# w_down by Strassen's seven products with weight sums made in DRAM, tanh gates, and differential heads in natural layout

## The chip, the cores and the metric

The kernel runs on one core of a Trainium2 chip. The metric is the device time of one execution in microseconds. Before the change it is 731.5 us, the median of 3 runs (731.49 to 732.18).

The engines are called by their short names in quoted rows: PE is TensorE (matmuls and transposes; PEld its weight loads, which overlap the matmuls), DVE is VectorE, ACT is ScalarE, POOL is GpSimd, SP only issues transfers. Every engine works through its instructions in order and waits at each for what that instruction needs.

## The reference

One decoder layer in float32 on x of shape (1, 512, 1024):

```
h = RMSNorm(x)
z = h @ w_in  ->  SWA q,k,v | differential q,k,v | gate logits gA, gB
yA = sliding-window attention (window 128, 8 heads, sinks)
ob[h] = (softmax(q1 k1) - lam * softmax(q2 k2)) @ v       4 heads of 128 columns, causal
yB = RMSNorm(ob) * subln * (1 - lam_init)                 per token and head
merged = sigmoid(gA) * (yA @ w_br_a) + sigmoid(gB) * (yB @ w_br_b)
x = x + merged @ w_o
u = causal depthwise conv3(RMSNorm(x) @ w_up) + b         2 x 2816 channels
x = x + (silu(ug) * uv) @ w_down                          2816 -> 1024
```

## The kernel before

Every operand of a large matmul is split in two parts, a high part rounded to the format that TensorE multiplies in one pass (fp32r) and the low rest. `mm3` (L143) issues three matmuls for a product of two blocks of 128: high x high, high x low, low x high. Weights are stored as units of 128 x 1024 in one DRAM tensor, in the order in which they are used (`worder`, L128). `wunit` (L135) keeps one unit ahead of the one in use: `split_unit` (L118) loads 512 KB through SP's queue into one of three buffers `raw`, ACT writes the high part `whi` and VectorE or POOL the low part `wlo`, both in three buffers. So a unit's split waits until TensorE has finished with the unit three before it, and its load waits until the split of the unit three before it is done.

TensorE's order is written out by hand (`manual_schedule`). In attention a stream of dense matmuls (gates, projections for the differential heads, branch A) is put between the steps of the attention units; the table `FILL` (L63) says how many steps of the stream follow each. The order of ACT, VectorE and POOL comes from the scheduler of the framework.

Four places matter here.

Gates. `gate(c)` (L465) evacuates a block of gate logits. `sigmoids` (L485) then applies the sigmoid to eight blocks at once; the first eight are held behind the last operations of sliding-window attention, the other eight behind the last exponentials of the differential heads. ACT keeps one set of function tables, and Sigmoid and Exp are in different ones: a load of tables stands before each change. `br_a` (L475) and `mix` (L848) multiply by the gates.

Differential heads. There are 16 units of a head and a block of 128 queries. `diff_score` makes the difference of the two softmaxes, `diff_trans` transposes it into one wide buffer for each head, and `diff_av` (L717) makes the product of a whole head, with the features on the partitions: twelve matmuls of 512 to 256 columns. The RMS norm over the features is then a sum over partitions: `token_sums` (L168) makes it with small matmuls against ones, and `along_free` (L183) spreads the factor over the partitions with eight diagonal matrices and two matmuls.

The up projection. 44 chunks of 128 channels, each from one weight unit of 24 matmuls; `conv` (L912) evacuates a chunk, applies the convolution, and after each pair of chunks the SiLU and the product, whose high part ACT writes and whose low part POOL.

The down projection (L965 to L974). Eight chunks of 128 output features; each takes three weight units and 22 products of `mm3` over 512 tokens, except that the last chunk is done in two halves of 256 tokens. VectorE adds x1, the residual, which lies with features on partitions, and ACT issues the store.

Of the kernel before, what the change touches and what calls it, by code (L numbers as in the profile page):

```python
# [11 lines left out]
F32 = mybir.dt.float32  # L12
# [46 lines left out]
U_N = U_DN + 8 * 3  # L59
# [3 lines left out]
FILL = dict(v=[9, 17, 25, 33], m=[0, 0, 0, 0], r=[4, 9, 13, 18], o=[7, 11, 15, 17], e=[1, 1, 0, 40], kv=4, up=3,  # L63
            warm=8, q=7, k=19, k2=4, s1=[0, 3, 2, 2, 2, 3, 3, 0, 0, 3], s2=[4, 3, 0, 3, 1, 7, 5, 2, 0, 1],
            s3=[3, 0, 1, 5, 6, 2, 2, 6, 0, 1], p0=4, p1=5, p2=8, ud=6, pd=[8, 9], f=[9, 0],
            a=[5, 1, 8, 7, 10, 2, 0, 3, 0, 1, 7, 4, 6, 0, 0, 5],
            b=[6, 2, 4, 4, 2, 7, 2, 1, 2, 0, 2, 0, 1, 1, 2, 2], c=[7, 0, 0, 1], d=[1, 0, 0, 5])
# [5 lines left out]
def tile_decoder_layer(ctx: ExitStack, tc: tile.TileContext, x4, wall, cst_d, relb_d, oneh_d, xn_d, out):  # L73
# [44 lines left out]
    def split_unit(i, width, eng):  # L118
        raw = wraw.tile([P, 1024], F32, tag="raw", name=nm("raw"))
        nc.sync.dma_start(raw[:, :width], wall[i][:, :width])  # L120
# [6 lines left out]

    worder = [u + i for u, n in ((U_QA, 4), (U_KV, 2), (U_GATE, 3), (U_DA, 4), (U_GATE + 3, 5), (U_VB, 4), (U_BRA, 4),  # L128
                                 (U_DB, 4), (U_GATE + 8, 8), (U_BRB, 4), (U_WO, 8), (U_UP, 2 * NF), (U_DN, 24))
              for i in range(n)]  # L130
    pooled = {u + i for u, n in ((U_DA, 4), (U_VB, 4), (U_DB, 4), (U_BRA, 4), (U_GATE, 16), (U_BRB + 3, 1)) for i in range(n)}
# [3 lines left out]
    def wunit(u):  # L135
        while wnext[0] < len(worder) and wnext[0] <= worder.index(u) + AHEAD:
            v = worder[wnext[0]]
            width = (DFF - 2 * 1024) if v >= U_DN and (v - U_DN) % 3 == 2 else 1024
# [4 lines left out]
    def mm3(ps, a, b, start, stop):  # L143

        nc.tensor.matmul(ps, a[0], b[0], start=start, stop=False)  # L145
        nc.tensor.matmul(ps, a[0], b[1], start=False, stop=False)  # L146
        nc.tensor.matmul(ps, a[1], b[0], start=False, stop=stop)  # L147
# [281 lines left out]
    def k_parts(ps, g):  # L429
# [5 lines left out]
        for k, (s, _) in zip(kh, halves):  # L435
            nc.scalar.activation(k[s, :], ps[s, :], AF.Copy, scale=g[s])
        for k, l, (s, o) in zip(kh, kl, halves):
            nc.vector.tensor_copy(k[o, :], k[s, :].bitcast(F32))
# [26 lines left out]
    def gate(c):  # L465
# [6 lines left out]
        nc.vector.tensor_tensor(t, ps, rbc, ALU.mult)  # L472
        G[c] = t

    def br_a(cp):  # L475
        w = wunit(U_BRA + cp)
        for j in range(2):
# [5 lines left out]
            nc.vector.tensor_tensor(G[c], ps, G[c], ALU.mult)  # L483

    def sigmoids(c0):  # L485
        return [nc.scalar.activation(G[c], G[c], AF.Sigmoid) for c in range(c0, c0 + 8)]
# [71 lines left out]
    swa_acts = []  # L558

    def swa_score(b, n):  # L560
# [22 lines left out]
        swa_acts.append(nc.scalar.activation(sk, sk, AF.Exp))  # L583
# [3 lines left out]
        for j in range(4):  # L587
            nc.vector.tensor_scalar(s[:, j, :W], s[:, j, :W], rc[:, j:j + 1], None, ALU.mult)
# [17 lines left out]
    def swa_av(b, n):  # L606
# [13 lines left out]
        if n == 1:  # L620
            qsl = slice(b * P, (b + 1) * P)
            uv = u.rearrange("p (j q) -> p j q", j=4)
            swa_acts.append(nc.scalar.activation(yah[:, :, qsl], uv, AF.Copy))
# [35 lines left out]
    exps = []  # L659

    def diff_score(h, b):
# [20 lines left out]
        for c in range(2):  # L682
            exps.append(nc.scalar.activation(p[:, c, :N], p[:, c, :N], AF.Exp, bias=nmx[:, c:c + 1],
                                             accum_out=sm[:, c:c + 1]))
# [3 lines left out]
        nc.vector.tensor_scalar(p[:, 1, :N], p[:, 1, :N], rc[:, 1:2], None, ALU.mult)  # L688
# [3 lines left out]
    def diff_trans(h, b):  # L692
        p = dp.pop((h, b))
        if b == 0:


            ath = at3.tile([P, 1664], F32R, tag="ath", name=nm("ath"), bufs=1)
            atl = at3.tile([P, 1664], F32R, tag="atl", name=nm("atl"), bufs=1)
            nc.gpsimd.memset(ath[:, 1408:1536].bitcast(F32), 0.0)
# [360 lines left out]
```

## Time and profile before

| what | us |
|---|---|
| median of 3 runs | 731.5 |
| the profiled execution | 730.34 |
| its span, first to last instruction | 728.6 |
| TensorE busy | 705.9 (97%) |
| VectorE busy | 450.0 (62%) |
| ACT busy | 316.0 (43%) |
| POOL busy | 167.0 (23%) |
| mean granted clock of TensorE | 0.993 |

The profile is of one execution. Its stages by TensorE's rows: projections and sliding-window attention to about 133 us, differential heads to about 303, gating and the output projection to about 345, the up projection to 603.9, the down projection to the end. A matmul's duration in a row is longer than the distance to the next start, since matmuls are pipelined. A line such as L145 belongs to the helper `mm3`, so the rows name the stage by the operand: xg is the normalised input, g, qv, y and act hold the activations of the down projection.

### The profile page before, as it was taken

Reading aid. Unit: us, or ns where it says so; the run is one execution under the profiler, and the core shown is the slowest. Engines: PE = TensorE matmul, PEld = TensorE weight load, DVE = VectorE, ACT = ScalarE, POOL = GpSimd, SP = SyncE. Lnnn points to the kernel's source line nnn. Section 1 sums busy time; section 2 is a strip of 40 time slices with the busy share of each in tenths; the row PEclk is TensorE's granted clock in tenths of the full one; section 3 lists DMA queues with packets and bytes.
Section 4 is the critical chain, followed back from the end, with each engine's and each line's share of the span. In section 5 each row is a group of like instructions: output and inputs, shape, how many; then the busy total and the mean of one; then the engine's idle time right before and its main releaser. Section 6 shows DMA issues by size and latency. Waiting matters only on the chain.

```text
span 728.6 us, 8960 instructions
## 1 busy us (share of the span) xinstructions
PE 705.9 (97%) x3312; PEld 582.6 (80%) x3312; DVE 450.0 (62%) x940; ACT 316.0 (43%) x522; POOL 167.0 (23%) x130
## 2 busy tenths in 40 slices
PE   8999999789999999989999999999999999999998
PEld 5888788668887778768888888888888888888888
DVE  5787797737429898685448877676676674322220
ACT  6554666854236446334426444444444442121220
POOL 1145253254446220274300210110110110000000
PEclk9999999989999999999999999999999999999999
DMA  8762202032221110235421332323323223333310
GB/s 315 289 207 88 87 30 88 0 116 87 72 99 62 58 59 30 87 107 167 132 87 58 116 117 91 111 86 96 107 87 102 101 80 101 125 107 108 109 66 30
DMA packets 21820, 74.04 MB, mean 102 GB/s; under 512 B 2612, under 2 KB 3152, under 8 KB 21648
## 3 DMA queue, kind: packets, MB, share of 16 engines
q1 hardware_dynamic: 18976, 65.02, 26.4%
q0 software_dynamic: 1360, 6.34, 2.6%
q10 hardware_dynamic: 1440, 2.11, 0.8%
q8 instruction: 26, 0.43, 0.2%
q14 instruction: 18, 0.15, 0.1%
HBM read 71.34 MB, written 4.47 MB: 104 GB/s over the span
## 4 chain that ended last, share of the span: by engine, by line
PE 78%; DVE 8%; issue 2%; ACT 2%; POOL 0%; DVEq 0%; ACTq 0%; POOLq 0%
PE pj L145 24%; PE pj L147 24%; PE pj L146 24%; PE at L725 1%; DVE g L850 1%; PE at L597 1%; PE at L444 1%; DVE g L849 1%; DVE o L193 1%; PE at L443 1%; DVE p L678 1%; DVE p L689 1%; PE at L705 1%; PE at L614 0%; DVE wlo L124 0%
## 5 line engine op out<-in xcount | busy, mean ns | idle before, releaser
L123 ACT ACTIVATE whi<-raw 128x1024 fp32r<-128x1024 f32 (+1 forms) x117 | 121.8, 1044 | 174.8 <-PE pj L146 115.9
L145 PE MATMUL pj<-xg,whi 128*128 128x512 f32 x480 | 189.6, 395 | 0.0
L147 PE MATMUL pj<-xg,wlo 128*128 128x512 f32 x480 | 187.3, 390 | 0.0
L146 PE MATMUL pj<-xg,whi 128*128 128x512 f32 x480 | 187.2, 390 | 0.0
L124 DVE TENSOR_TENSOR wlo<-raw,whi 128x1024 fp32r<-128x1024 f32 (+1 forms) x84 | 103.4, 1234 | 81.9 <-ACT whi L123 81.8
L147 PEld LDWEIGHTS pj<-xg,wlo 128*128 128x128 f32 x480 | 90.2, 188 | 19.2
L146 PEld LDWEIGHTS pj<-xg,whi 128*128 128x128 f32 x480 | 90.4, 188 | 17.7
L145 PEld LDWEIGHTS pj<-xg,whi 128*128 128x128 f32 x480 | 90.3, 188 | 17.5
L124 POOL TENSOR_TENSOR wlo<-raw,whi 128x1024 fp32r<-128x1024 f32 x33 | 79.6, 2418 | 96.2 <-ACT whi L123 86.7
L145 PE MATMUL pj<-whi,xg 128*128 128x512 f32 (+1 forms) x156 | 59.5, 382 | 6.0 <-ACT whi L123 5.9
L916 DVE TENSOR_TENSOR u<-pj,rbc 128x512 f32<-128x512 f32 x44 | 30.2, 689 | 48.3 <-PE pj L147 48.3
L146 PE MATMUL pj<-wlo,xg 128*128 128x512 f32 (+1 forms) x156 | 58.2, 373 | 1.7 <-POOL wlo L124 1.7
L147 PE MATMUL pj<-whi,xg 128*128 128x512 f32 (+1 forms) x156 | 58.1, 372 | 0.1
L145 PEld LDWEIGHTS pj<-whi,xg 128*128 128x128 f32 x156 | 29.8, 191 | 11.3 <-ACT whi L123 6.0
L919 ACT ACTIVATE yc<-u,cst 128x512 f32<-128x512 f32 x44 | 35.5, 810 | 4.5 <-DVE u L916 4.5
L145 PE MATMUL pj<-y,whi 128*128 128x512 f32 (+1 forms) x95 | 37.0, 390 | 0.0
L147 PE MATMUL pj<-y,wlo 128*128 128x512 f32 (+1 forms) x95 | 36.3, 382 | 0.2 <-POOL wlo L124 0.2
L147 PE MATMUL pj<-qv,wlo 128*128 128x512 f32 (+1 forms) x94 | 35.4, 377 | 1.1 <-DVE wlo L124 1.1
L146 PE MATMUL pj<-y,whi 128*128 128x512 f32 (+1 forms) x95 | 36.2, 381 | 0.0
L921 DVE SCALAR_TENSOR_TENSOR yc<-u,cst,yc 128x510 f32<-128x510 f32 x44 | 34.8, 794 | 1.3
L146 PEld LDWEIGHTS pj<-wlo,xg 128*128 128x128 f32 x156 | 29.9, 191 | 7.0 <-POOL wlo L124 2.2
L145 PE MATMUL pj<-qv,whi 128*128 128x512 f32 (+1 forms) x94 | 35.4, 376 | 0.0
(213 smaller groups left out, 1151.3 us busy)
## 6 DMA issues: line engine op xcount, KB each, us to landing
raw<-in_w_dram SPq DMA_DIRECT2D x109, 512.0 KB, 3.3
raw<-in_w_dram SPq DMA_DIRECT2D x8, 384.0 KB, 3.1
scr<-scr POOLq DMA_DIRECT2D x1, 2304.0 KB, 11.4
xnat<-in_xn_dram SPq DMA_DIRECT2D x2, 1024.0 KB, 9.4
tmp<-in_x_dram POOLq DMA_DIRECT2D x8, 256.0 KB, 3.2
g<-in_x_dram SPq DMA_DIRECT2D x7, 256.0 KB, 6.7
out_dram<-x ACTq DMA_DIRECT2D x7, 256.0 KB, 2.0
bias_a<-scr POOLq DMA_DIRECT2D x1, 1024.0 KB, 7.3
```

The costliest lines, as they stand in the source:

```text
L123: nc.scalar.activation(hi[:, :width], raw[:, :width], AF.Copy)
L124: eng.tensor_tensor(lo[:, :width], raw[:, :width], hi[:, :width].bitcast(F32), ALU.subtract)
L145: nc.tensor.matmul(ps, a[0], b[0], start=start, stop=False)
L146: nc.tensor.matmul(ps, a[0], b[1], start=False, stop=False)
L147: nc.tensor.matmul(ps, a[1], b[0], start=False, stop=stop)
L193: nc.vector.tensor_scalar(dg[:, t * P:(t + 1) * P], ident, part[:, t:t + 1], None, ALU.mult)
L443: nc.tensor.matmul(ps, q[:, qsl], kh[:, ksl], start=True, stop=False)
L444: nc.tensor.matmul(ps, q[:, qsl], kl[:, ksl], start=False, stop=True)
L597: nc.tensor.transpose(ps[:, j * P:(j + 1) * P], s[:, j, kb * P:(kb + 1) * P], ident)
L916: nc.vector.tensor_tensor(u, ps, rbc2, ALU.mult)
L919: nc.scalar.activation(y, u, AF.Identity, bias=cst[:, C_CB + ch:C_CB + ch + 1], scale=cw[2])
L921: nc.vector.scalar_tensor_tensor(y[:, 2:S], u[:, 0:S - 2], cw[0], y[:, 2:S], ALU.mult, ALU.add)
```

## The change

It has three parts, and `FILL` has other numbers.

**w_down as seven half-size products.** The activations (512 x 2816) and w_down (2816 x 1024) are cut into quarters: tokens, hidden channels and output columns in halves. Strassen's scheme in its form with chained sums needs seven products of 256 x 1408 x 512 instead of eight. Four of the seven right-hand sides are sums of quarters of w_down, T1 to T4. They are made in DRAM during the up projection: ACT issues 24 copies of 512 KB from DRAM to DRAM (two behind each of chunks 4 to 9, one behind each of chunks 14 to 19 and 24 to 29), and POOL issues 24 accumulating transfers of 512 KB that add a quarter to a copy. (The weights of the other three products are quarters as they are; the signs are such that only additions of quarters are needed.) The sums of activations are made by POOL in `combine`, four operations of half width for every two pairs of chunks; the order of the chunks is changed (`F_ORDER`) so that pairs f and f + 11 follow each other. The split of activations into high and low parts moves from the up projection into the down projection (`split_left`: ACT and VectorE, 256 columns at a time).

The down projection now has tokens on the partitions: a block of 128 x 128 activations is the stationary operand and 512 columns of weights stream. A weight unit holds 2 x 512 columns (the sixth of a product one), and feeds 12 (or 6) matmuls. x1 is turned into natural layout by 32 transposes on TensorE and eight copies on ACT during the first product. Outputs are stored in natural layout, so the host no longer transposes them.

**Tanh gates.** sigmoid(z) = (1 + tanh(z/2)) / 2. The tanh is applied by ACT as each gate block is evacuated, the 1 is added in the multiplication by the gate, and the half in the residual after w_o. Tanh is used under the same tables as Exp: the new order has two table loads (the first one and one for SiLU) where the old one has five.

**Differential heads in natural layout.** The product of each unit is made on its own with queries on partitions: 3 x (b + 1) matmuls of 128 columns for query block b, 30 for a head. The sum of squares comes out of ACT's evacuation, the factor is applied per partition, and four transposes for each head turn the result. Half of the scalings in the softmaxes, and the second copies of the keys, move from VectorE to ACT.

```diff
+    def sum_copy(t, src, u):
+        nc.scalar.dma_start(tsum[t - T1][u], wall[U_DN + 6 * src + u] if src < T1 else tsum[src - T1][u])
+    def sum_add(t, src, u):
+        nc.gpsimd.dma_start(tsum[t - T1][u], wall[U_DN + 6 * src + u], accum_op=ALU.add, max_dma_last_dim=4096)
+    copies = {4 + u: [(T1, R12, u), (T3, R12, u)] for u in range(6)}
+    copies.update({14 + u: [(T2, T1, u)] for u in range(6)})
+    copies.update({24 + u: [(T4, T2, u)] for u in range(6)})
+    adds = [(T1, R11, u) for u in range(6)] + [(T3, R22, u) for u in range(6)]
+    adds = {1: adds[:3], 2: adds[3:8], 3: adds[8:]}
+    adds.update({4: [(T2, R22, u) for u in range(3)], 5: [(T2, R22, u) for u in range(3, 6)],
+                 6: [(T4, R21, u) for u in range(2)], 7: [(T4, R21, u) for u in range(2, 6)]})
...
         t = g_slot(F32)
         nc.vector.tensor_tensor(t, ps, rbc, ALU.mult)
+        nc.scalar.activation(t, t, AF.Tanh, scale=0.5)
         G[c] = t
...
-            nc.vector.tensor_tensor(G[c], ps, G[c], ALU.mult)
-    def sigmoids(c0):
-        return [nc.scalar.activation(G[c], G[c], AF.Sigmoid) for c in range(c0, c0 + 8)]
+            nc.vector.scalar_tensor_tensor(G[c], G[c], 1.0, ps, ALU.add, ALU.mult)
...
-    def diff_av(h):
...
+    def diff_av(h, b):
...
+        po = at()[:, :P]
         for i, (part, at_) in enumerate(((0, ath), (1, ath), (0, atl))):
+            for kb in range(b + 1):
+                nc.tensor.matmul(po, at_[:, kb * P:(kb + 1) * P], vb[kb][part][:, h * P:(h + 1) * P],
+                                 start=i == 0 and kb == 0, stop=i == 2 and kb == b)
+        ob = o[:, b * P:(b + 1) * P]
+        nc.scalar.activation(ob, po, AF.Square, accum_out=ss[:, b:b + 1])
+        nc.scalar.activation(ob, po, AF.Copy)
...
     def diff_out(h):
-        r = along_free(col, otile, lambda: fs.fill(FILL["m"][h]))
...
+        for b in range(NT):
+            nc.tensor.transpose(ps[:, b * P:(b + 1) * P], o[:, b * P:(b + 1) * P], ident)
...
+    def combine(f):
+        a, b = act["F", f], act["F", f + NH]
...
+        nc.gpsimd.tensor_tensor(s1, a[:, hi_t], b[:, hi_t], ALU.subtract)
+        nc.gpsimd.tensor_tensor(s3, a[:, lo_t], a[:, hi_t], ALU.subtract)
+        nc.gpsimd.tensor_tensor(s2, s1, a[:, lo_t], ALU.subtract)
+        i = nc.gpsimd.tensor_tensor(s4, b[:, lo_t], s2, ALU.add)
+        with tc.issue_after(i.ins):
+            for piece in adds.get(f, ()):
+                sum_add(*piece)
...
+    def product(op, banks, first):
+        n0 = steps.index((op, 0))
+        for u in range(6):
+            n = n0 + u
+            w = wunit(U_DN + 6 * op + u)
+            if n + 1 < len(steps) and n > 0:
+                split_left(n + 1)
+            a = lefts.pop(n)
+            for t in range(2):
+                for j in range(2 if u < 5 else 1):
+                    mm3(banks[t], [a[i][:, 256 * j + P * t:256 * j + P * t + P] for i in range(2)],
+                        [w[i][:, 512 * j:512 * j + 512] for i in range(2)],
+                        start=first and u == 0 and j == 0, stop=u == 5, skip=not first)
+            if op == DN_ORDER[0] and u > 0:
+                for i in range(8 * (u - 1) // 5, 8 * u // 5):
+                    x1_natural(i // 2, i % 2)
```

In the new kernel `mm3` is at L172 to L174, the weight split at L131 and L132, the tanh at L502, the head products at L744 and the transposes of x1 at L1024.

ACT where the projection of the differential values begins: before, the parts of the first heads (qv), the sigmoids (g), then the second weight unit of that projection.

```order
L436 ACTIVATE qv_1587<-at_1580,cst 64x512
L436 ACTIVATE qv_1588<-at_1580,cst 64x512
L486 ACT_TABLE_LOAD
L486 ACTIVATE g_666<-g_666 128x512
...
L486 ACTIVATE g_1526<-g_1526 128x512
L123 ACTIVATE whi_1611<-raw_1609 128x1024
L683 ACT_TABLE_LOAD
```

The same place of the changed kernel: the first two units of the projection, then the parts, then the third unit.

```order
L131 ACTIVATE whi_1615<-raw_1613 128x1024
L502 ACTIVATE g_1417<-g_1417 128x512
...
L131 ACTIVATE whi_1645<-raw_1643 128x1024
...
L451 ACTIVATE qv_1558<-at_1553,gqa 64x512
...
L465 ACTIVATE qv_1600<-at_1592,cst 64x512
L131 ACTIVATE whi_1715<-raw_1713 128x1024
L711 ACTIVATE p_1655,dsm_1657<-p_1655,dnmx_1666 128x128 x2
```

The sigmoids and both table loads are gone from between the parts and the weights, and two units instead of one stand ahead of the parts.

TensorE in the first product of the changed down projection, at the end of the second unit (al and xg hold activations, at_5501 and at_5502 are the two banks of the product, x_ are blocks of x1):

```order
L172 MATMUL at_5502<-whi_5507,al_5449 128x512
L173 MATMUL at_5502<-wlo_5508,al_5449 128x512
L174 MATMUL at_5502<-whi_5507,al_5450 128x512
L1024 MATMUL at_5547<-ident,x_697_3378 128x128
L1024 MATMUL at_5547<-ident,x_701_3387 128x128
L1024 MATMUL at_5547<-ident,x_710_3429 128x128
L1024 MATMUL at_5547<-ident,x_719_3471 128x128
L172 MATMUL at_5501<-whi_5525,xg_5529 128x512
```

Groups of four transposes come between units of the first product; the next unit's weights and activations are other tiles.

VectorE at the change from the first product to the second (eyc is the evacuation of the first product's banks at_5501 and at_5502; xg_5666 is the low part of the second product's first activations):

```order
L132 TENSOR_TENSOR wlo_5698<-raw_5695,whi_5697 128x1024
L1057 TENSOR_TENSOR eyc_5691<-at_5501,xg_5552 128x512
L982 TENSOR_TENSOR xg_5666<-g_3841,xg_5665 128x256
L982 TENSOR_TENSOR xg_5666<-g_4009,xg_5665 128x256
L1057 TENSOR_TENSOR eyc_5693<-at_5502,xg_5590 128x512
L132 TENSOR_TENSOR wlo_5722<-raw_5719,whi_5721 128x1024
```

The low part for the second product stands behind the evacuation of the first bank, which waits for the first product's last unit.

More of the change, by code (lines that the diff above doesn't have):

```diff
@@ L798, in tile_decoder_layer @@
         if i > 0:
-            products(2 * i)
+            for u, hb in enumerate(todo):
+                if u < len(todo) - 1 and max(u + 2, FILL["v0"]) == i:
+                    fs.until("vb")
+                    diff_av(*hb)
+                    fill("c", u)
             diff_trans(*todo[i - 1])
             fill("b", i - 1)
-            products(2 * i + 1)
+            if i == len(todo):
+                diff_av(*todo[-1])
         for step, at_unit in ((diff_rms, FILL["r"]), (diff_out, FILL["o"])):
@@ L918, in conv @@
         cw = [cst[:, C_CW + 3 * ch + i:C_CW + 3 * ch + i + 1] for i in range(3)]
-        nc.scalar.activation(y, u, AF.Identity, bias=cst[:, C_CB + ch:C_CB + ch + 1], scale=cw[2])
+        i = nc.scalar.activation(y, u, AF.Identity, bias=cst[:, C_CB + ch:C_CB + ch + 1], scale=cw[2])
+        with tc.issue_after(i.ins):
+            for piece in copies.get(c, ()):
+                sum_copy(*piece)
         nc.vector.scalar_tensor_tensor(y[:, 1:S], u[:, 0:S - 1], cw[1], y[:, 1:S], ALU.mult, ALU.add)
@@ L962, in tile_decoder_layer @@
         full(c, wunit(U_UP + c), 0, NK, xn, conv)
[L965 to L974 removed]
+        if c >= 2 * NF - 3 and c < 2 * NF - 1:
+            split_left(c - 2 * NF + 3)
@@ new lines, in temp, with store @@
+    def temp(tag, bufs):
+        return ffn.tile([P, S], F32, tag=tag, name=nm("e" + tag), bufs=bufs)
+    def store(i, j, t, v):
+        nc.scalar.dma_start(out[(2 * i + t) * P:(2 * i + t + 1) * P, j * S:(j + 1) * S], v)
+    chain, n5 = [at(), at()], [at(), at()]
+    product(R11, chain, True)
+    p1, us, n5s, ws = [], [], [], []
+    for t in range(2):
+        p1.append(temp("yc", 4))
+        nc.vector.tensor_tensor(p1[t], chain[t], x1n[2 * t], ALU.add)
+    product(T1, n5, True)
+    for t in range(2):
+        n5s.append(temp("u", 3))
+        nc.vector.tensor_tensor(n5s[t], n5[t], x1n[2 * (2 + t) + 1], ALU.add)
@@ new lines, in tile_decoder_layer @@
+    product(T2, chain, False)
+    for t in range(2):
+        us.append(temp("yc", 4))
+        nc.vector.tensor_tensor(us[t], chain[t], x1n[2 * t + 1], ALU.subtract)
+    p2 = [at(), at()]
+    product(R21, p2, True)
+    for t in range(2):
+        nc.vector.tensor_tensor(p1[t], p2[t], p1[t], ALU.add)
+        store(0, 0, t, p1[t])
+    product(T3, chain, False)
+    for t in range(2):
+        nc.vector.tensor_tensor(n5s[t], n5s[t], chain[t], ALU.subtract)
+        store(1, 1, t, n5s[t])
+    product(R22, n5, False)
@@ L977, in _bucket_onehot @@
+    for t in range(2):
+        nc.vector.tensor_tensor(us[t], n5[t], us[t], ALU.subtract)
+        store(0, 1, t, us[t])
+    product(T4, chain, False)
+    for t in range(2):
+        v = x1n[2 * (2 + t)]
+        nc.vector.tensor_tensor(v, chain[t], v, ALU.add)
+        store(1, 0, t, v)
 def _bucket_onehot():
```

201 lines of the change are left out of this document (103 added, 98 removed).

## The prediction

> **What bounds the kernel now.** I read the page of the profile first, then busy time by stretch, then TensorE's instructions in order of time at the two places where its starts are not evenly spaced. On the page I look at the shares of the engines, at what the chain of waits consists of, and at what the split of the weights waits for:
>
> ```profile
> span 728.6 us, 8960 instructions
> ...
> PE 705.9 (97%) x3312; PEld 582.6 (80%) x3312; DVE 450.0 (62%) x940; ACT 316.0 (43%) x522; POOL 167.0 (23%) x130
> ...
> PE 78%; DVE 8%; issue 2%; ACT 2%; POOL 0%; DVEq 0%; ACTq 0%; POOLq 0%
> ...
> L123 ACT ACTIVATE whi<-raw 128x1024 fp32r<-128x1024 f32 (+1 forms) x117 | 121.8, 1044 | 174.8 <-PE pj L146 115.9
> ...
> L124 DVE TENSOR_TENSOR wlo<-raw,whi 128x1024 fp32r<-128x1024 f32 (+1 forms) x84 | 103.4, 1234 | 81.9 <-ACT whi L123 81.8
> ```
>
> TensorE is the bound, and the weights are ready before they are needed: ACT's split waits 115.9 us in all for a buffer that TensorE still reads. The columns of the next view are the stretch, its length, then busy us (and instructions) of PE, PEld, DVE, ACT, POOL, the granted clock, the DMA share and GB/s:
>
> ```profile
> 80.00:120.00 40.00, 38.46 (x198) 32.13 (x197) 34.09 (x108) 27.83 (x73) 16.99 (x11) 1.00 0.20 65
> 120.00:160.00 40.00, 32.42 (x160) 26.93 (x159) 22.71 (x59) 26.56 (x51) 15.96 (x13) 0.91 0.16 53
> 450.00:500.00 50.00, 50.00 (x222) 41.42 (x221) 33.43 (x41) 22.34 (x28) 5.21 (x4) 1.00 0.30 102
> 650.00:700.00 50.00, 50.00 (x221) 41.18 (x220) 13.01 (x13) 9.24 (x10) 0.00 (x0) 1.00 0.34 116
> ```
>
> The up and down projections are pure TensorE. The loss is in attention, most of it between 120 and 160 us. A matmul's duration overlaps the next one's, so I price by the distance of starts:
>
> ```profile
> 603.89 0.39 PE L145 MATMUL pj<-g,whi 128*128 128x512 f32 x1
> ...
> 605.93 0.39 PE L145 MATMUL pj<-g,whi 128*128 128x512 f32 x1
> ...
> 720.00 0.28 PE L145 MATMUL pj<-qv,whi 128*128 128x256 f32 x1
> ...
> 721.80 0.28 PE L145 MATMUL pj<-qv,whi 128*128 128x256 f32 x1
> ...
> 724.90 0.28 PE L147 MATMUL pj<-act,wlo 128*128 128x256 f32 x1
> ```
>
> Nine starts of 512 columns in 2.04 us are 0.227 us each; fifteen of 256 columns in 1.80 us are 0.120 us. The down projection runs from 603.89 to 724.90.
>
> **The down projection.** Before: seven chunks of 66 matmuls of 512 columns and one of 132 of 256, 462 x 0.227 + 132 x 0.120 = 120.7 us (the rows say 121.1 with the last one). After: seven products of 11 x 2 x 3 = 66 matmuls of 512 columns, the same 462, so 104.8 us; the 132 go. New on TensorE are 32 transposes of 128x128 that turn x1 into natural layout. The price of an instruction of 128 columns is in these rows, first of the chain of waits (x8 in one piece), then in order of time:
>
> ```profile
> 94.38 0.87 PE at L597 x8
> ...
> 241.37 0.88 PE at L705 x4
> ...
> 290.32 1.97 PE at L725 x12
> ...
> 140.29 0.22 PE L443 MATMUL at<-qv,qv 128*128 128x128 f32 x1
> 140.35 0.28 PE L444 MATMUL at<-qv,qv 128*128 128x128 f32 x1
> ```
>
> 0.87 / 8 = 0.109 us when they follow each other; the bounds are 0.06 (the closest pair of starts) and 0.22 (0.88 / 4). I take 0.109, the row with the longest run: 32 x 0.109 = 3.5 us. At the change of the first product to the second, VectorE's new order has the evacuation of the first product ahead of the low part that the second product needs at its third matmul. That evacuation ends about where TensorE ends, and two low parts of 256 columns follow at 0.42 us each (the row of the tail, below): about 0.7 us. Later changes have the parts ready. Sum 109.0, so **-12.1 us**.
>
> The pieces that have to keep up with it, from ACT's groups:
>
> ```profile
> L581 ACT ACTIVATE s<-s,nmx 128x256 f32<-128x256 f32 (+1 forms) x32 | 15.0, 475 | 20.1 <-DVE nmx L576 15.9 <-issue 4.2
> ...
> L424 ACT ACTIVATE qv<-at,gqa 64x512 fp32r<-64x512 f32 x16 | 10.9, 681 | 4.5 <-PE at L415 4.3
> ```
>
> Per unit of weights TensorE now takes 12 x 0.227 = 2.72 us where it took 5.44. What must keep up: ACT 1.04 + two left splits of 256 columns at about 0.48 (an estimate from the exponential of 256 columns, 475 ns a piece), 2.0 us; VectorE 1.23 + 2 x 0.42 = 2.1 us; a load of 512 KB in three buffers. A buffer's round is 3.3 landing + 1.04 + 1.23 = 5.6 us of the 8.2 us of three units. All three lie under 2.72 us, so I cost the feed at nothing; its cover is 2.6 us of landing time.
>
> **The weight sums.** 24 copies and 24 accumulating transfers of 512 KB run during the up projection, where nothing waits for TensorE's feed (windows above: DMA share 0.30). The rows for transfers:
>
> ```profile
> raw<-in_w_dram SPq DMA_DIRECT2D x109, 512.0 KB, 3.3
> scr<-scr POOLq DMA_DIRECT2D x1, 2304.0 KB, 11.4
> bias_b<-scr POOLq DMA_DIRECT2D x1, 512.0 KB, 7.8
> ...
> 32.00:36.00 4.00, 4.00 (x36) 4.00 (x35) 3.90 (x19) 0.17 (x1) 1.66 (x1) 1.00 0.93 344
> ```
>
> The last row holds the DRAM-to-DRAM transfer of scr beside weights: 344 GB/s at share 0.93, 370 at full share, so 512 KB cost 1.42 us of all sixteen engines. The last copy that depends on a sum is issued by ACT at chunk 29, the first at chunk 4: 25 chunks x 5.44 = 136 us. In that time go 25 weights, 24 copies and 18 sums: 69.6 us + 18 a, with a for one sum. At a = 1.42 that is 95 us; at twice this (source and destination are both read) 121 us. Either fits in 136, and a late copy blocks ACT's next weight split only after 8.6 us more (two chunks less the 2.3 us of the split). So nothing, until a passes 4.2 us; from there each us costs 18. No row shows an accumulating transfer: below, 1.42; above, the slowest landing of 512 KB, 7.8 us, 65 us of delay. I take twice the copy, because the sum is the same stream with a second read. The Trainium skill, in Collectives: The Full Stack, Part 3 (why ReduceScatter is half of AllGather), speaks against the change here: an add in a DMA engine needs two source reads on one ring and goes at half a copy's rate. By that rule the sum stays as it is, and the margin shrinks from 41 to 15 us.
>
> On the engines the up projection gets lighter or stays: ACT loses 22 copies and gains 24 issues, POOL does 44 half-width operations for 22. Nothing.
>
> **Tanh gates.** The two blocks of sigmoids with their table loads go. The first is on the path:
>
> ```profile
> 140.18 1.28 ACT L486 ACT_TABLE_LOAD   x1
> ...
> 140.57 0.27 PE L444 MATMUL at<-qv,qv 128*128 128x128 f32 x1
> ...
> 141.48 4.26 ACT L486 ACTIVATE g<-g 128x512 f32<-128x512 f32 x8
> ...
> 146.74 0.79 PE L145 MATMUL pj<-whi,xg 128*128 128x512 f32 x1 [5.89 <-ACT whi L123]
> ...
> 149.22 0.79 PE L146 MATMUL pj<-wlo,xg 128*128 128x512 f32 x1 [1.69 <-POOL wlo L124]
> ...
> 152.25 0.40 PE L147 MATMUL pj<-whi,xg 128*128 128x512 f32 x1
> ```
>
> TensorE stands from 140.68 to 146.74, 6.1 us; the next start is 2.48 us later instead of 0.23, 2.2 us lost; and seven starts to 152.25 take 3.03 us instead of 1.59, 1.4 us lost while the clock recovers. Together 9.7 us. In the new order two weight units of this projection stand ahead of the head parts on ACT, and the third is needed 48 x 0.227 = 10.9 us of matmuls later, while twelve half-height copies at 0.68 us (L424's row; 8.2 us) stand before it. So the stall should go; I take **-9.0**, between -4 (the third unit late by half) and -9.7. Tanh itself costs the 0.53 us of a sigmoid, one by one behind the gates, hidden by matmuls. The second block of sigmoids (286 to 295 us) delayed nobody by the list of waits: 0.
>
> **Heads in natural layout.** Removed from TensorE: 4 x 1.97 = 7.9 us of products (L725), 8 x 0.227 = 1.8 of L194, 16 sums over partitions. One of these costs what two triples lie apart beyond 0.68 us:
>
> ```profile
> 293.76 0.39 PE L147 MATMUL pj<-y,wlo 128*128 128x512 f32 x1
> 293.99 0.28 PE L173 MATMUL at<-ones,o 128*128 128x2 f32 x2
> ...
> 294.68 0.40 PE L147 MATMUL pj<-y,wlo 128*128 128x512 f32 x1
> ```
>
> 0.92 - 0.68 = 0.24 us, 3.8 in all: -13.5. Added: 4 x 30 products of 128 columns and 16 transposes, 136 x 0.109 = 14.8 us (8 to 30 by the bounds). Net **+1.3**. Fewer columns, but as many weight loads as before.
>
> **Other stalls.** The list of TensorE's waits has a few us in attention, all for VectorE or ACT:
>
> ```profile
> PE at L597 <- DVE s L588: 1.5, 1, 1.5
> ...
> PE at L705 <- DVE p L689: 1.3, 2, 1.0
> ...
> PE at L194 <- DVE o L193: 0.7, 1, 0.7
> ```
>
> VectorE loses the diagonals (L193) and half of several scalings; ACT gains those, at 27.8 of 40 us busy already between 80 and 120. I take **-1**, between -5 (all go) and +9 (ACT late wherever VectorE was).
>
> **Tail.** Before, the last evacuation is half a chunk; now a whole one:
>
> ```profile
> 709.45 0.69 DVE L973 TENSOR_TENSOR x<-pj,x 128x512 f32<-128x512 f32 x1 [2.02 <-PE pj L147]
> ...
> 725.22 0.42 DVE L973 TENSOR_TENSOR x<-pj,x 128x256 f32<-128x256 f32 x1 [7.46 <-PE pj L147]
> ...
> out_dram<-x ACTq DMA_DIRECT2D x7, 256.0 KB, 2.0
> ```
>
> 0.69 - 0.42, and the first half's evacuation just before it: **+0.4**. The store lands as fast.
>
> Sum: -12.1 - 9.0 + 1.3 - 1.0 + 0.4 = -20.4 us. The profiled execution took 730.3 us, which gives 709.9; the median shown is 1.2 higher, so I predict **711 us**. On its own this case spans 706 to 716.
>
> **Rivals.**
> *ACT becomes late in attention* (0.20). For it: 27.8 of 40 us busy, and about 30 us more work moved to it up to 305 us; also each block's product now needs its own accumulation bank. Against it: VectorE, at 34.1 of 40, was the one waited for more often, and is relieved. The gain of the sigmoids is given back: 711 + 9 = 720, reaching from 716 to 724.
> *The sums are slow* (0.06), the other side: ACT, in order, waits at the copy of T2 into T4 for an accumulating transfer, and the weight split behind it starves TensorE. It decides from a = 4.2 us, cancels the gain at 4.2 + 20.4 / 18 = 5.3 us, and at 7.8 us gives 776. Against it: twice the price of a copy is 2.8 us, far from 5.3.
> *The feed limits the down projection* (0.06): 42 units by a third of a buffer's round. It decides where landing passes 5.2 us (three average units of 104.8 / 42 are 7.5 us, less 2.3 of ACT and VectorE), gives 3.08 us a unit and no gain at 6.9, and 743 at the 7.8 of bias_b. Against it: 116 GB/s now, 193 needed, 344 seen.
> *More than forecast* (0.06): all listed stalls go and those of the mixing stage with them, 703.
> *The sums or products do not shorten TensorE's work at all*: the 462 matmuls are counted in the new order, so only a slower start distance could do it (0.02).
>
> **How the numbers follow.** The forecast has 0.60. With the first rival and the fourth, 702 to 724 holds a little over 8 of 10. Faster by over 0.2% (what a measurement of this kernel can tell from no change): 0.60 + 0.20 + 0.06 and a mild part of the two late-transfer cases, 0.90; within it 0.02; slower 0.08.
>
> **What would show it.** The last 109 us with starts 0.227 us apart and 32 transposes in the first product; no wait for ACT near 140 us and no clock under 1 there; landing of the accumulating transfers near 3 to 5 us, and no wait of ACT for them; starts 0.11 us apart in the new head products. Wrong, if TensorE idles in the up or down projection, or if its idle time in attention exceeds that of before less 9 us.

## The result, and the profile after

The changed kernel takes **711.5 us** (median of 4 runs, 711.15 to 712.85) against 731.8 us before (4 runs beside it): a ratio of 0.972, 95% interval 0.971 to 0.974. The prediction was 711. The profiled execution took 711.55 us, its span is 709.8. Runs of one kernel here spread by 0.4 to 3.9 us, the longer ones mostly with the lower mean clock of TensorE, so differences of one microsecond are read from the traces and not from the medians.

The page of the changed kernel, shares of the engines and of the chain that ended last:

```profile
span 709.8 us, 9203 instructions
...
PE 692.6 (98%) x3260; PEld 571.9 (81%) x3260; DVE 478.8 (67%) x962; ACT 370.6 (52%) x690; POOL 197.0 (28%) x168
...
PE 83%; DVE 8%; ACT 6%; issue 1%; DMA 1%; SPq 0%; DVEq 0%; ACTq 0%
```

TensorE is still the bound; it has 13 us less to do, and ACT has 55 us more. Busy time by stretch of the changed kernel, columns as in the prediction:

```profile
120.00:160.00 40.00, 37.89 (x189) 31.01 (x188) 25.79 (x62) 28.28 (x57) 16.59 (x11) 1.00 0.19 63
...
450.00:500.00 50.00, 50.00 (x222) 41.39 (x221) 35.55 (x41) 19.82 (x24) 19.20 (x22) 1.00 0.91 261
...
650.00:700.00 50.00, 50.00 (x222) 41.42 (x221) 37.85 (x60) 29.32 (x53) 0.00 (x0) 1.00 0.68 211
```

Between 120 and 160 us TensorE now does 189 instructions where it did 160, at a clock of 1.00 instead of 0.91. Between 450 and 500 us the DMA engines are 0.91 busy (0.30 before) and TensorE does not notice.

Three marks divide the time: the last stall before the up projection, the first matmul of the down projection, and the last matmul. TensorE of the changed kernel in order of time, the last stall first, then a stall in the up projection that the kernel before does not have, then the two ends of the down projection:

```profile
314.94 0.50 PE L174 MATMUL pj<-qv,wlo 128*128 128x512 f32 x1 [1.10 <-DVE wlo L132]
...
399.88 0.40 PE L173 MATMUL pj<-xg,whi 128*128 128x512 f32 x1
401.72 0.50 PE L174 MATMUL pj<-xg,wlo 128*128 128x512 f32 x1 [1.45 <-DVE wlo L132]
...
597.24 0.39 PE L172 MATMUL at<-whi,al 128*128 128x512 f32 x1
...
705.47 0.39 PE L174 MATMUL at<-whi,xg 128*128 128x512 f32 x1
```

and the first mark in the kernel before:

```profile
323.35 0.51 PE L147 MATMUL pj<-qv,wlo 128*128 128x512 f32 x1 [1.09 <-DVE wlo L124]
```

| part, by the profiled executions | before | after | moved | predicted |
|---|---|---|---|---|
| start to the last stall before the up projection | 323.4 | 314.9 | -8.4 | -8.7 |
| from there to the first matmul of the down projection | 280.5 | 282.3 | +1.8 | 0 |
| down projection, first to last start | 121.0 | 108.2 | -12.8 | -12.1 |
| last start to the end of the span | 3.7 | 4.3 | +0.6 | +0.4 |

Stage by stage the sum looks right. Whether the terms inside the first row were right the two traces cannot say, since tanh, heads, copies and the numbers of the order all act there. That is what most of the experiments are for.

### The profile page after: what moved, and what is told of

Same layout as the page of the kernel before. It is cut to its first block, busy times and chain, and to the rows that moved or that the text cites. A ratio compares the mean times of both kernels' runs of the same rounds, so it can differ in the third digit from the quotient of the medians.

```text
span 709.8 us, 9203 instructions
## 1 busy us (share of the span) xinstructions
PE 692.6 (98%) x3260; PEld 571.9 (81%) x3260; DVE 478.8 (67%) x962; ACT 370.6 (52%) x690; POOL 197.0 (28%) x168
## 3 DMA queue, kind: packets, MB, share of 16 engines
q0 software_dynamic: 4816, 18.92, 12.1%
## 4 chain that ended last, share of the span: by engine, by line
PE 83%; DVE 8%; ACT 6%; issue 1%; DMA 1%; SPq 0%; DVEq 0%; ACTq 0%
PE pj L174 21%; PE pj L172 21%; PE pj L173 21%; PE at L174 5%; PE at L172 5%; PE at L173 5%; PE at L744 1%; DVE g L866 1%; DMA g<-in_x_dram 1%; PE at L472 1%; DVE qv L453 1%; DVE wlo L132 1%; ACT p L711 1%; PE at L471 1%; PE at L626 1%
## 5 line engine op out<-in xcount | busy, mean ns | idle before, releaser
L131 ACT ACTIVATE whi<-raw 128x1024 fp32r<-128x1024 f32 x135 | 139.4, 1035 | 153.0 <-PE pj L173 98.3
L172 PE MATMUL pj<-xg,whi 128*128 128x512 f32 x480 | 189.2, 394 | 0.0
L174 PE MATMUL pj<-xg,wlo 128*128 128x512 f32 x480 | 187.4, 390 | 1.4 <-DVE wlo L132 1.4
L132 DVE TENSOR_TENSOR wlo<-raw,whi 128x1024 fp32r<-128x1024 f32 x102 | 125.1, 1228 | 37.9 <-ACT whi L131 37.5
L132 POOL TENSOR_TENSOR wlo<-raw,whi 128x1024 fp32r<-128x1024 f32 x33 | 79.5, 2411 | 119.5 <-ACT whi L131 113.9
L174 PEld LDWEIGHTS pj<-xg,wlo 128*128 128x128 f32 x480 | 90.2, 188 | 21.0 <-DVE wlo L132 1.9
L172 PEld LDWEIGHTS pj<-xg,whi 128*128 128x128 f32 x480 | 90.4, 188 | 17.9
L172 PE MATMUL pj<-whi,xg 128*128 128x512 f32 (+1 forms) x156 | 58.5, 375 | 1.4 <-ACT xg L286 1.4
L174 PE MATMUL pj<-whi,xg 128*128 128x512 f32 (+1 forms) x156 | 57.6, 369 | 0.1
L172 PE MATMUL at<-whi,xg 128*128 128x512 f32 x146 | 57.3, 392 | 0.0
L174 PE MATMUL at<-whi,xg 128*128 128x512 f32 x146 | 56.9, 390 | 0.0
L173 PE MATMUL at<-wlo,xg 128*128 128x512 f32 x146 | 56.8, 389 | 0.0
L966 ACT ACTIVATE yc<-yc 128x512 f32<-128x512 f32 x22 | 13.9, 632 | 45.5 <-DVE yc L961 45.1
L960 DVE SCALAR_TENSOR_TENSOR yc<-u,cst,yc 128x511 f32<-128x511 f32 x44 | 35.6, 810 | 1.7 <-ACT yc L956 1.7
L172 PEld LDWEIGHTS pj<-whi,xg 128*128 128x128 f32 x156 | 29.5, 189 | 6.5 <-ACT xg L286 1.8
L174 PEld LDWEIGHTS pj<-whi,xg 128*128 128x128 f32 x156 | 29.4, 189 | 5.6 <-DVE xg L287 0.5
## 6 DMA issues: line engine op xcount, KB each, us to landing
tsum<-in_w_dram POOLq DMA_DIRECT2D x24, 512.0 KB, 11.4
```

Source lines behind the costliest of these rows:

```text
L131: nc.scalar.activation(hi[:, :width], raw[:, :width], AF.Copy)
L132: eng.tensor_tensor(lo[:, :width], raw[:, :width], hi[:, :width].bitcast(F32), ALU.subtract)
L172: nc.tensor.matmul(ps, a[0], b[0], start=start, stop=False, skip_group_check=skip)
L173: nc.tensor.matmul(ps, a[0], b[1], start=False, stop=False, skip_group_check=skip)
L174: nc.tensor.matmul(ps, a[1], b[0], start=False, stop=stop, skip_group_check=skip)
L960: nc.vector.scalar_tensor_tensor(y[:, 1:S], u[:, 0:S - 1], cw[1], y[:, 1:S], ALU.mult, ALU.add)
```

## The experiments

Every kernel here computes the whole reference. All medians stand beside runs of the kernel before on the same chip (731.2 to 731.9 us), and ratios are to it. The kernels ran on more than one chip, so between two of them some tenths of a microsecond can be the chip's.

### One part at a time

Four kernels: Strassen with its weight sums alone, the attention edits alone, tanh alone, and Strassen with tanh. The edits are the parts of the diff above; the numbers of the order (`FILL`) are the old ones except in the second. For tanh alone, its main lines:

```diff
+        nc.scalar.activation(t, t, AF.Tanh, scale=0.5)
         G[c] = t
...
-            nc.vector.tensor_tensor(G[c], ps, G[c], ALU.mult)
+            nc.vector.scalar_tensor_tensor(G[c], G[c], 1.0, ps, ALU.add, ALU.mult)
...
-        for i in sigmoids(0):
-            sig.enter_context(tc.issue_after(i.ins))
```

> The kernel before with only the down projection and the weight sums of the change; sigmoid blocks, head layout and order of attention as before. Theory (the terms of the sum add up): the down projection's -12.1 and the tail's +0.4 come alone, -11.7, 720 us; with what the trace of the changed kernel shows instead (-12.8 in the down stage, +0.6 in the tail, +1.8 of a new stall near 400 us in the up projection) -10.4, 721.4 us, and the stall is there too. Rival A (the stall near 400 us belongs to the attention edits, which move work of ACT behind the start of the up projection): no stall, 719.7 us. Rival B (part of the gain of the changed kernel hangs on the attention edits): above 724 us.

> The changed kernel with the old down projection and without weight sums: tanh gates, heads in natural layout, the new order of attention. Theory: -9.0 + 1.3 - 1.0 = -8.7 as forecast, or the -8.4 that the two traces show up to the last stall before the up projection: 723.1 to 723.5 us; no stall near 400 us. Rival A (that stall belongs to the attention edits): it stays, 725 us.

> The kernel before with tanh in place of the two blocks of sigmoids, nothing else; heads and the table of the order as before. Theory: the stall at 140 us goes with its after-effects, -9.0 (between -4 and -9.7), 722.8 us; the granted clock is 1.00 between 120 and 160 us. Rival (the old order was fitted to the sigmoid block, the weight unit and the head parts now stand in ACT's queue in another place and half of the stall stays): -4, 727.8 us.

> The changed kernel with the head layout, the ACT scalings and the order of attention of the kernel before: new down projection, weight sums and tanh only. Theory: the heads' +1.3 and the -1.0 of other stalls leave again, 0.3 less than the changed kernel, 711.2 us. Rival (the natural layout is worth more than its TensorE work says, since it takes the diagonals and half of the scalings from VectorE): 714 to 716 us. Rival (it is worth less: ACT is late for its copies, as in the 2.4 us at 266 us): 708.5 us.

| kernel | median us | ratio, 95% interval |
|---|---|---|
| Strassen alone | 720.7 | 0.985 (0.983 to 0.987) |
| attention edits alone | 722.0 | 0.987 (0.985 to 0.989) |
| tanh alone | 728.6 | 0.9965 (0.995 to 0.998) |
| Strassen and tanh | 718.3 | 0.982 (0.980 to 0.984) |

Strassen alone is worth 11.2 us and the attention edits alone 9.9; together 21.1, and the changed kernel has 20.4. So the two halves add up. The new stall in the up projection belongs to Strassen: with the attention edits alone TensorE waits for nothing between 350 and 420 us, and the rows of Strassen alone have it:

```profile
409.07 0.39 PE L172 MATMUL pj<-xg,whi 128*128 128x512 f32 x1
410.92 0.50 PE L173 MATMUL pj<-xg,wlo 128*128 128x512 f32 x1 [1.46 <-DVE wlo L131]
```

Tanh alone missed: 3.3 us, not 9.0, and not even the 4 of the rival. The granted clock between 120 and 160 us missed too: it is 0.91, as in the kernel before, where 1.00 was expected. Beside Strassen tanh is worth 2.4. So the heads and the order hold 6.8 us (718.3 to 711.5), where the prediction had +0.3 for heads and other stalls. TensorE of tanh alone in order of time (the traced execution took 730.1 us):

```profile
142.69 0.28 PE L444 MATMUL at<-qv,qv 128*128 128x128 f32 x1
143.42 0.30 PE L443 MATMUL at<-qv,qv 128*128 128x128 f32 x1 [0.45 <-DVE qv L439]
...
147.24 0.28 PE L444 MATMUL at<-qv,qv 128*128 128x256 f32 x1
149.06 0.36 PE L443 MATMUL at<-qv,qv 128*128 128x256 f32 x1 [1.53 <-DVE qv L439]
...
149.84 0.39 PE L147 MATMUL pj<-whi,xg 128*128 128x512 f32 x1
151.95 0.47 PE L703 MATMUL at<-ident,p 128*128 128x128 f32 x1 [1.72 <-DVE p L687]
```

The six microseconds in which TensorE waited for ACT's weight split are gone. In their place it waits for VectorE three times within ten microseconds: for the low parts of the keys twice, and for the first softmax of the differential heads. VectorE in the same kernel, and POOL beside it:

```profile
138.84 1.51 DVE L426 SCALAR_TENSOR_TENSOR qv<-at,gqa,qv 64x512 fp32r<-64x512 f32 x2 [1.77 <-ACT qv L424]
...
144.85 2.10 DVE L438 CAST qv<-qv 64x512 fp32r<-64x512 f32 x1
...
147.72 0.42 DVE L438 CAST qv<-qv 64x512 fp32r<-64x512 f32 x1
...
144.27 2.40 POOL L124 TENSOR_TENSOR wlo<-raw,whi 128x1024 fp32r<-128x1024 f32 x1 [2.04 <-issue]
```

From 138.84 to 148.9 VectorE has no pause. That suggested a theory: the three moves from VectorE to ACT, which were written down as a side effect of the heads, are what frees this place. The rows allow another one. The same cast takes 2.10 us beside a subtraction of POOL and 0.42 without, and the difference of 1.7 us is about as large as the longer wait for the low parts (1.53 us). The last section has more on this; a kernel with POOL's subtraction elsewhere was not tried.

### The moves from VectorE to ACT

Added to tanh alone, and undone in the changed kernel:

```diff
+        for k, (s, o) in zip(kh, halves):
+            nc.scalar.activation(k[o, :], ps[s, :], AF.Copy, scale=g[s])
-            nc.vector.tensor_copy(k[o, :], k[s, :].bitcast(F32))
...
+            if j % 2:
+                nc.scalar.activation(s[:, j, :W], s[:, j, :W], AF.Copy, scale=rc[:, j:j + 1])
...
+        nc.scalar.activation(p[:, 1, :N], p[:, 1, :N], AF.Copy, scale=rc[:, 1:2])
-        nc.vector.tensor_scalar(p[:, 1, :N], p[:, 1, :N], rc[:, 1:2], None, ALU.mult)
```

> The kernel before with tanh and the three moves of copies and scalings from VectorE to ACT (the second halves of the differential keys, every second scaling of the window heads, the scaling of the second map); heads and numbers of the order as before. With tanh alone TensorE still lost 7.7 us between 130 and 160 us, now behind VectorE (its run from 138.84 to 148.9 without a pause holds four copies of keys, one of 2.10 us), where the changed kernel loses 3.0. Theory (VectorE's list there is what held, the moves are what frees it): about 4.5 less than tanh alone, 724 us, and no wait for the low part of the keys. Rival (the natural head layout or the new numbers of the order bring the 6.8 us that lie between the changed kernel and the one with Strassen and tanh only): within 1 us of tanh alone, 728 us.

> The changed kernel with these three moves undone, all on VectorE again. Theory: the 4.5 come back, 716 us. Rival (the layout or the numbers bring the gain): 712 us or less. Second rival (ACT is the later one in the changed attention stage, 2.2 us of wait for it at 266 us): faster than 711 us.

Tanh with the moves takes 730.6 us (0.9987, 0.9975 to 0.9999), 2 us more than tanh alone. The changed kernel without them takes **710.2 us** (0.971, 0.970 to 0.972; 709.95 to 710.78), about 1 us less than with them. In both pairs the two intervals overlap, so no cost of the moves is shown; but the gain of 4.5 us that the theory asked for is missing on both sides. The waits for the low parts did shrink, but in tanh with the moves TensorE then ran sooner into the next one:

```profile
147.46 0.39 PE L147 MATMUL pj<-whi,xg 128*128 128x512 f32 x1
151.16 0.33 PE L707 MATMUL at<-ident,p 128*128 128x128 f32 x1 [3.31 <-DVE p L691]
```

In this softmax too VectorE stands beside POOL: its negation of two columns of maxima, at 146.88, takes 2.04 us where it takes 0.17 in tanh alone, and ends when a subtraction of POOL does. How much of the theory's gain that hides was not tried.

And in the changed kernel ACT is the later of the two engines at 268 us, as the second rival said: the wait for `ath`, 2.22 us there (first row, the changed kernel), is 1.04 without the moves (second, line numbers shifted by four).

```profile
268.84 0.66 PE L744 MATMUL at<-vbh,ath 128*128 128x128 f32 x4 [2.22 <-ACT ath L728]
```

```profile
268.24 0.66 PE L740 MATMUL at<-vbh,ath 128*128 128x128 f32 x4 [1.04 <-ACT ath L724]
```

Little comes of it: without the moves there are three new waits for VectorE between 220 and 300 us (0.65, 0.59 and 0.49 us), and all waits of TensorE in this stretch sum to 2.5 us with the moves and 2.7 without.

### The numbers of the order

What remained were the natural layout and the numbers in `FILL`, which say how many steps of the dense stream follow each step of attention. The same edit, backwards in the changed kernel and forwards in the kernel before and in tanh alone (the parts of the lines in which numbers change):

```diff
-s1=[0, 3, 2, 2, 2, 3, 3, 0, 0, 3], s2=[4, 3, 0, 3, 1, 7, 5, 2, 0, 1],
-s3=[3, 0, 1, 5, 6, 2, 2, 6, 0, 1], p0=4, p1=5, p2=8,
-a=[5, 1, 8, 7, 10, 2, 0, 3, 0, 1, 7, 4, 6, 0, 0, 5],
-b=[6, 2, 4, 4, 2, 7, 2, 1, 2, 0, 2, 0, 1, 1, 2, 2]
+s1=[0, 3, 0, 3, 2, 4, 4, 0, 0, 3], s2=[2, 3, 0, 5, 1, 7, 5, 5, 0, 0],
+s3=[3, 0, 2, 5, 6, 2, 2, 6, 0, 1], p0=4, p1=3, p2=10,
+a=[6, 1, 7, 8, 10, 2, 0, 5, 0, 2, 7, 3, 6, 0, 0, 5],
+b=[6, 2, 4, 4, 2, 7, 2, 1, 2, 2, 0, 0, 1, 4, 2, 2]
```

> The changed kernel with the old numbers of the order for the window heads (s1, s2, s3), the fills p1 and p2 and the pieces between scores and transposes (a, b); numbers that only the new head layout has are kept. Theory: numbers that move a few matmuls are worth about 1 us, 711 to 713 us. Rival (the order carries the gain of attention): 715 to 717 us.

> The kernel before with the changed kernel's numbers s1, s2, s3, p1, p2, a and b of the order, nothing else. With the old ones the changed kernel took 721.2 us in place of 711.5, 9.7 more. Theory (the numbers fill places that exist only where the sigmoid block is gone and the heads have their new shape): no gain here, 730 to 733 us; the stall for the weight at 140 us stays at about 6 us. Rival (the numbers are a better order for any of these kernels, and the 9.7 belong to them alone): 722 us.

> The kernel before with tanh and the new numbers, heads in the old layout. Theory (tanh takes the sigmoid block off ACT, and the new numbers then put matmuls where the first softmax of the differential heads would leave TensorE waiting; three triples of matmuls, 2.04 us, are what the stall at 148 us differs by, 3.48 and 1.44 us): the loss between 120 and 160 us falls from 7.7 to about 3.5, 724 us; the other half of the gain, at 250 to 290 us, needs the new head layout. Rival A (numbers and heads do it only together): 728 us or more. Rival B (the heads are worth nothing, tanh and numbers all): 721 us.

The last two columns are TensorE's lost time in two stretches, from the distances of its starts: what each exceeds 0.227, 0.172, 0.120 or 0.109 us by, for 512, 384, 256 and 128 columns (good to some tenths).

| kernel | median us | ratio | lost 120-160 | lost 220-300 |
|---|---|---|---|---|
| before (sigmoids, old heads, old numbers) | 731.8 | | 9.8 | 6.6 |
| before, new numbers | 743.2 | 1.016 (1.014 to 1.017) | 12.3 | 15.3 |
| tanh, old heads, old numbers | 728.6 | 0.9965 | 7.7 | 6.3 |
| tanh, old heads, new numbers | 733.2 | 1.003 (1.002 to 1.004) | 2.1 | 15.4 |
| changed kernel, old numbers | 721.2 | 0.986 (0.984 to 0.988) | 9.6 | 9.8 |
| changed kernel | 711.5 | 0.972 | 3.0 | 5.3 |

So the numbers are worth 9.7 us in the changed kernel and cost 11.5 us in the kernel before and 4.6 in tanh alone. "About 1 us" missed widely, and so did "no gain" for the kernel before, which became slower. The expectation for tanh with new numbers was half right: the first stretch falls to 2.1 as expected, and needs no new heads; the second loses 9 more. At 148 us the mechanism can be counted. The changed kernel with the old numbers:

```profile
147.49 0.39 PE L174 MATMUL pj<-whi,xg 128*128 128x512 f32 x1
151.20 0.47 PE L727 MATMUL at<-ident,p 128*128 128x128 f32 x1 [3.32 <-DVE p L717]
```

and with its own:

```profile
148.77 0.39 PE L174 MATMUL pj<-whi,xg 128*128 128x512 f32 x1
150.44 0.33 PE L727 MATMUL at<-ident,p 128*128 128x128 f32 x1 [1.28 <-DVE p L717]
```

`p2` went from 8 to 10 and `a[0]` from 5 to 6: three more steps of three matmuls, 2.04 us, before the transposes that wait for the first softmax. The wait is 2.04 us shorter. TensorE waits for the same thing, but has more to do meanwhile. The stream is finite, so these steps are missing later. With the old heads they are missed where the keys of the third head are made and where the factor of a head goes through VectorE's diagonals (tanh with new numbers):

```profile
230.86 0.39 PE L147 MATMUL pj<-xg,wlo 128*128 128x512 f32 x1
234.43 0.48 PE L443 MATMUL at<-qv,qv 128*128 128x128 f32 x1 [3.18 <-DVE qv L438]
...
288.18 0.80 PE L194 MATMUL at<-o,ones 128*128 128x512 f32 x1 [1.52 <-DVE o L193]
```

The new heads have neither the diagonals (L193) nor the wait for them, so there the steps can be spared. The layout of the heads and the numbers earn their gain together: with the old numbers the heads and their moves to ACT cost 2.9 us (718.3 to 721.2). How far the old heads would come with numbers fitted to tanh was not tried.

### The stall in the up projection, and the weight sums

The twelve first copies issued by SP behind weight loads in attention; then the same with the moves to ACT undone; then every accumulating transfer doubled:

```diff
-        nc.scalar.dma_start(tsum[t - T1][u], wall
+        (nc.sync if src < T1 else nc.scalar).dma_start(tsum[t - T1][u], wall
...
+            if v in early:
+                sum_copy(*early[v])
             wnext[0] += 1
```

```diff
     def sum_add(t, src, u):
         nc.gpsimd.dma_start(tsum[t - T1][u], ... accum_op=ALU.add, max_dma_last_dim=4096)
+        nc.gpsimd.dma_start(extra[u], ... accum_op=ALU.add, max_dma_last_dim=4096)
```

> The changed kernel with the twelve copies of R12 into T1 and T3 issued by SP behind the loads of twelve weight units in attention instead of by ACT in the up projection; the other transfers as they are. Theory (the new stall of 1.6 us near 400 us is a late weight split: the copies take 1.3 us of ACT's time and stretch the weight's landing from 3.3 to 6.3 us): the stall goes, 1.6 less, 709.9 us. Rival (the stall comes from POOL's new half-width sums, in whose time VectorE's operations take 1.2 us where they took 0.75): it stays, 711.5 us.

> The changed kernel with the three moves from VectorE to ACT undone and the twelve early copies issued by SP in attention. Theory (both gains add up: 1.3 and the 1.6 of the stall near 400 us): 708.6 us. Rival (the early copies now slow the weight loads of attention, where VectorE has less room): 710 us or more.

> The changed kernel with every accumulating transfer of the weight sums followed by a second one of the same source into a spare piece of DRAM, so that a sum costs the sixteen engines twice as much. From the shares of POOL's queue one sum costs 2.8 us now (12.1% of 709.8 us against 2.6% of 728.6, 24 transfers). Theory (the budget of the prediction: 69.6 us + 18 a against 136 us and 8.6 us of room for the split): a = 5.6, 170.4 - 144.6 = 26 us of delay, 737 us, and ACT stands at its copies in the up projection. Rival (the queues of weights and copies get their share first and the sums run in what is left, with no copy late): within 2 us of the changed kernel, 713 us.

With the copies early the stall is gone; TensorE of that kernel where it stood:

```profile
399.81 0.39 PE L177 MATMUL pj<-xg,whi 128*128 128x512 f32 x1
400.04 0.39 PE L178 MATMUL pj<-xg,wlo 128*128 128x512 f32 x1
400.26 0.39 PE L176 MATMUL pj<-xg,whi 128*128 128x512 f32 x1
```

POOL's sums stand at the same place, so they are not the cause. Whether it is ACT's time for the issues or the longer landing of the weight was not told apart. The profiled execution is 1.8 us shorter (709.78 against 711.55), but two of its four runs are at 711.7 and 712.3, and the median of 710.7 (0.972, 0.970 to 0.975) shows no gain that could be told from none. With the moves undone as well it is 709.8 us (five runs, 708.94 to 711.78; 0.970, 0.969 to 0.971): the fastest kernel of these, though its interval still touches that of the changed kernel.

The weight sums themselves cost TensorE nothing, as forecast. Queues of the changed kernel, POOL's (q0) and ACT's (q10), with packets, MB and the share of sixteen engines; then its transfers with the median time to land:

```profile
q0 software_dynamic: 4816, 18.92, 12.1%
q10 hardware_dynamic: 2064, 14.70, 5.5%
...
tsum<-in_w_dram POOLq DMA_DIRECT2D x24, 512.0 KB, 11.4
...
tsum<-in_w_dram ACTq DMA_DIRECT2D x12, 512.0 KB, 5.9
tsum<-tsum ACTq DMA_DIRECT2D x12, 512.0 KB, 6.3
```

and the queues of the kernel before:

```profile
q0 software_dynamic: 1360, 6.34, 2.6%
q10 hardware_dynamic: 1440, 2.11, 0.8%
```

24 sums took 12.1% of 709.8 less 2.6% of 728.6 = 67 us of all engines, 2.79 each; 24 copies 33 us, 1.38 each. The prediction had 2.84 and 1.42. That an accumulating transfer costs two copies is also the rule that the prediction quoted from the Trainium skill, Collectives: The Full Stack, Part 3; the trace agrees, at a ratio of 2.0.

With the sums doubled the kernel takes 732.8 us (one run), its span 731.0. ACT's waits and TensorE's rows of that kernel:

```profile
ACT yc L971 <- DMA tsum<-in_w_dram: 31.4, 3, 18.5
```

```profile
514.38 0.39 PE L179 MATMUL pj<-xg,wlo 128*128 128x512 f32 x1
521.01 0.80 PE L177 MATMUL pj<-xg,whi 128*128 128x512 f32 x1 [6.24 <-ACT whi L131]
...
547.93 0.39 PE L179 MATMUL pj<-xg,wlo 128*128 128x512 f32 x1
550.75 0.50 PE L177 MATMUL pj<-xg,whi 128*128 128x512 f32 x1 [2.43 <-ACT whi L131]
```

That is the rival of slow sums, in its place: ACT stands 18.5 us at the first copy of T2 into T4, and TensorE runs out of weights behind it. Between 510 and 560 us it loses 16.6 us, where the budget said 26. The rest of the 21.2 us of the span lies elsewhere: about 3.4 of it before 80 us, where this kernel also fills its spare piece of DRAM (issued from 19 to 35 us), and about 1.4 between 220 and 300 us. The budget finds the mechanism and its place, and prices it too high by more than half.

## Why the prediction was right, and where only its sum was

*Down projection, -12.1: right, -12.8.* The 462 matmuls came 0.227 us apart, and the transposes of x1 took 3.1 us in place of 3.5. The 0.7 us at the change of products did not appear: VectorE did the low parts of the second product between the two evacuations of the first and not behind both, and eight transposes of x1 stood between the products on TensorE, 0.79 us from their start to the next matmul.

*Weight sums, 0: right on the sums, wrong on the copies.* A sum costs what was taken, no copy came late, and doubling them shows the wait that was named. The sign that was given for it was a poor one: the sums land after 11.4 us, not 3 to 5, since several stand in POOL's queue at once. What was left out is +1.6 us at 400 us: the first copies come while the convolutions of four chunks are still being caught up, and delay one weight split. "ACT loses 22 copies and gains 24 issues" compared totals, not the place. By the prediction's own sign, TensorE idle in the up projection, this step was wrong by a little.

*Feed of the down projection, 0: right.* TensorE has no wait there. ACT's splits of its units wait for TensorE to free a buffer, so weights were ahead; from ACT's waits in the changed kernel:

```profile
ACT whi L131 <- PE at L174: 17.1, 14, 1.7
```

*Tanh, -9.0: this step failed.* The stall for ACT's weight went, as described, and with tanh alone only 3.3 us came of it (2.4 beside Strassen), below the range of 4 to 9.7. The step asked what is late next on ACT, and found nothing. The next late thing was VectorE, with the keys and the first softmax, held up in part by POOL.

*Heads +1.3 and other stalls -1.0: this failed the other way.* On TensorE the heads' products cost what was said: 12 in 1.29 us, from the first of these rows of the changed kernel to the matmul after them, 0.107 each where 0.109 was taken. ("As many weight loads as before" is not so: 72 matmuls of the old heads in the program, 48 products, 8 of L194 and 16 sums, became 136. The price counted them and is right.)

```profile
288.13 0.56 PE L744 MATMUL at<-vbh,ath 128*128 128x128 f32 x4
...
288.97 0.61 PE L744 MATMUL at<-vbh,atl 128*128 128x128 f32 x4
289.42 0.45 PE L172 MATMUL pj<-y,whi 128*128 128x512 f32 x1
```

But heads and order together gave -6.8 beside Strassen and tanh, past the -5 of the range for other stalls. The term that is missing is the numbers of the order. The change was read as having them, and they were given no price; they are worth 9.7 us in the changed kernel.

So -9.0 and +0.3 were wrong by 6 to 7 us each, in opposite directions, and their sum, -8.7, was right within 0.3 us of the traced executions. That these two errors cancel is luck: nothing in the prediction ties one to the other. The sign that asked for 9 us less of idle time in attention was nearly met: TensorE's lost time up to 300 us, measured as in the table of the numbers, fell by 7.8 us, from 24.6 to 16.8. Most of it is one place: TensorE's lost time between 120 and 160 us fell from 9.8 to 3.0 us. The prediction gave this to tanh, which alone gets 2.1 of it; the rest comes with the numbers. Since numbers, heads and tanh need each other, their shares depend on the order in which they are added, and only the sum of the three is a measured gain.

*The rivals.* ACT late in attention: it is there, a wait of 2.2 us at 268 us, far from 9, and no part of the total is shown to be its, since other waits take its place when the moves are undone. The others did not occur, and slow sums occur when their price is doubled.

## What to carry to other kernels

In an order that is filled by hand, a wait that is removed is worth only the time until the next operand that is late; look for that on every engine, not only on the one that was waited for. Count the numbers that place filler work as an edit with a price of its own: the same numbers gained 9.7 us in one kernel and lost 11.5 in another, so a part tried without its numbers says little about its worth. Moving work to a less busy engine gains only where the fuller engine is the later one at that place. And before an engine is called full, compare its operations there with the same ones elsewhere: one that takes several times as long may be held by another engine.

## What the runs showed of the hardware

A small operation of VectorE can last as long as the operation that POOL has under way, and end with it. VectorE of the changed kernel: the negation of two columns of maxima, at two places and undisturbed at a third:

```profile
146.68 1.52 DVE L709 TENSOR_SCALAR dnmx<-dmx 128x2 f32<-128x2 f32 x1
...
151.10 2.35 DVE L709 TENSOR_SCALAR dnmx<-dmx 128x2 f32<-128x2 f32 x1
...
264.90 0.17 DVE L709 TENSOR_SCALAR dnmx<-dmx 128x2 f32<-128x2 f32 x1
```

POOL in the same kernel:

```profile
145.77 2.40 POOL L132 TENSOR_TENSOR wlo<-raw,whi 128x1024 fp32r<-128x1024 f32 x1 [5.64 <-issue]
151.02 2.40 POOL L132 TENSOR_TENSOR wlo<-raw,whi 128x1024 fp32r<-128x1024 f32 x1 [2.85 <-ACT whi L131]
```

POOL's operations end at 148.17 and 153.42, VectorE's at 148.20 and 153.45. The first of them is in the softmax that TensorE waits for at 148.77: 1.35 us of excess against a wait of 1.28 to 1.44. Of the sixteen negations in this kernel five begin well inside a subtraction of POOL; all five end 0.02 to 0.03 us behind it, and the others that meet no work of POOL take 0.15 to 0.17 us. Not every operation is held: the maxima of a block of scores, at 146.13, take 0.29 us inside the first of these subtractions, as they do in tanh alone without one. That the wait would go with POOL's split elsewhere was not tried. The Trainium skill, SBUF — State Buffer, Who interferes with whom, has a rule for it: VectorE shares its second pair of ports with POOL, an operation of VectorE that uses both of its pairs, as a copy, a cast or a tensor_scalar can, contends for it, and whoever comes second stands until the other's instruction is done. These rows agree with it.
